# Down products as pairs of column blocks, seven products in the first chunk of each, and one hand-made order for the FFN layer of a decoder trunk

## The chip, the cores and the metric

The kernel runs on one core of a Trainium2 chip. The metric is the device time of one execution in microseconds. TensorE multiplies, VectorE and ScalarE work on tiles in SBUF and PSUM, GpSimd does a few small operations and issues the accumulating transfers, SyncE (SP) issues most loads. Each engine has its own queue of instructions and takes them in order; an instruction may first wait for counts of other engines or transfers.

## The reference

Two layers over a sequence of 256 tokens of width 2048, in float32. The first mixes with retention heads and a short convolution, the second with differential attention; each ends in a SwiGLU feed-forward layer (FFN) of hidden width 5632:

```
def swiglu(h, w_gate, w_up, w_down):
    return (jax.nn.silu(h @ w_gate) * (h @ w_up)) @ w_down
...
x = x + swiglu(rms_norm(x, norm_ffn[layer]), ffn_w_gate[layer], ffn_w_up[layer], ffn_w_down[layer])
```

## The kernel before

A float32 product is made of three float32r matmuls: each operand is split into a high part `hi` (a cast on ScalarE) and a low part `lo = src - hi` (VectorE), and hi x hi, lo x hi and hi x lo are summed in PSUM. `split_w` does it for weights, two k-tiles of 512 columns at a time (128x1024 elements), into a pool of four buffers.

The FFN runs in three parts of 4, 4 and 3 blocks of 512 hidden columns. For each part `gate_up` makes the hidden columns, then a down stage multiplies them by their rows of `w_down` and adds to `x_sb`.

`gate_up` treats gate and up weights as a 2x2 arrangement: the two token halves (a1, a2) and the two halves of a chunk of four k-tiles on one side, gate and up columns on the other. Each block of 512 columns goes through four chunks c = 0..3 of kinds 7, 8, 7, 8 (`KINDS`). In a chunk of kind 8 the four weight operands w11, w21, w12, w22 meet two activation operands each, 4 x 2 x 2 x 3 = 48 matmuls. In a chunk of kind 7 a Strassen-like scheme takes seven products (`SEVEN`), 7 x 2 x 3 = 42 matmuls, and pays with sums: of weights (t1 made by an accumulating transfer that GpSimd issues, t2, t3, t4 by VectorE, L240 to L244), of activations (s1 to s4, made once in `Stream.quad`), and of results. The results stand in PSUM tiles b1 to b7; b3 and b5 are the two banks of one tile `p35`.

Its order is written by hand (`manual_schedule`): a list of slots, one for each weight operand. In each slot the split of the operand three slots on is issued (`prepare(i + AHEAD)`), then the matmuls, then what `gather` has set for this slot: `copies`, `inner`, `gates`, `silu`, `ups` and `hidden`, which take the results to the hidden block `gs`. Eight slots after a block's last, `hidden` finishes it and appends a job; in chunk 1 of the next block the slots w21, w12 and w22 call `step()`, which moves the job on: `splits` transposes the block on TensorE and splits it from PSUM (`split4`, L361 on ScalarE, L362 on VectorE) into `hi` and `lo`, the activations of the down stage.

A down stage is four calls of `col_block`, for 512 output columns each: per k-tile, three matmuls for each token half into one of two accumulators, then `add_residual`. Nothing is summed but the accumulators. Its order, and that of all code outside `manual_schedule`, comes from a scheduler at build time. `Stream.quad` prepares a quarter of the normalized x; for the last quarter of each FFN's norm it runs as a job in chunk 1 of the first block, followed by `squares` and `scale`. Names in rows: f01 is block 1 of layer 0's FFN, 2w11 the operand w11 of its chunk 2, d00o0 column block 0 of the down stage of layer 0's part 0, n1_c3 quarter 3 of that FFN's norm.

Of the kernel before, what the change touches and what calls it, by code (L numbers as in the profile page):

```python
# [35 lines left out]
def decoder_trunk(ctx: ExitStack, tc: tile.TileContext, a: dict):  # L36
# [149 lines left out]
    def gate_up(layer, wg, wu, st, r, p0, p1, hi, lo):  # L186
# [3 lines left out]


        kinds = st.kinds
        nc_ = len(kinds)
        last7 = max(c for c, kind in enumerate(kinds) if kind == 7)
        last8 = max(c for c, kind in enumerate(kinds) if kind == 8)
        chunks = [(b, c) for b in range(p0, p1) for c in range(nc_)]
        tiles, banks, sums, begun = {}, {}, {}, set()
# [50 lines left out]
        def get_banks(b):  # L248
            nm = f"f{layer}{b}_"
            for i in (1, 2, 6, 4):  # L250
                banks[b, f"b{i}"] = acc_tile(f"{nm}p{i}")
            banks[b, "b7"] = tp_tile(nm + "p7")
            b35 = psum.tile([P, 2, NB], F32, tag="sc", name=nm + "p35")
            banks[b, "b3"], banks[b, "b5"] = b35[:, 0], b35[:, 1]
# [18 lines left out]

        later = {}

        def gather(i):


            n, b, c, operand, _ = slots[i]
            nm = f"f{layer}{b}"  # L280

            def at(k, f):
                later.setdefault(i + k, []).append(f)

            if c == last7 and operand == "t3":
                u = work.tile([P, NT, NB], F32, tag="u", name=nm + "u", bufs=1)
                g = work.tile([P, NT, NB], F32, tag="gs", name=nm + "gs", bufs=1)
                sums[b] = u, g

                def copies():  # L290
                    nc.scalar.copy(u[:, 0], banks[b, "b1"])
                    nc.scalar.copy(g[:, 0], banks[b, "b1"])

                def inner():
                    nc.vector.tensor_tensor(u[:, 0], banks[b, "b6"], u[:, 0], ALU.subtract)
                    nc.vector.tensor_tensor(u[:, 1], banks[b, "b7"], u[:, 0], ALU.add)

                at(2, copies)
                at(4, inner)
            if c == nc_ - 1 and operand == "w21":  # L300
                u, g = sums[b]

                def gates():
                    nc.vector.tensor_tensor(g[:, 0], banks[b, "b2"], g[:, 0], ALU.add)
                    nc.vector.tensor_tensor(g[:, 1], banks[b, "b4"], u[:, 1], ALU.subtract)
# [590 lines left out]
```

## Time and profile before

| what | value |
|---|---|
| median of 3 runs | 2184.47 us (2183.98 to 2184.51) |
| the profiled execution | 2184.89 us, span 2183.1 us |
| busy share of the span: PE, DVE, ACT, POOL | 99%, 75%, 53%, 8% |
| matmuls and transposes on PE | 9851 records |
| granted clock over the span | 1.00 |

PE is TensorE, DVE VectorE, ACT ScalarE, POOL GpSimd. The span runs from the first to the last instruction on the core. A busy share is an average over stages; matmuls are pipelined, so a record of 0.39 us may start 0.23 us after the one ahead of it. A bracket behind a row gives the idle time of the engine before it, and what ended it.

### The profile page before, as it was taken

How to read it: one execution, taken by the hardware profiler on the slowest of the kernel's cores; microseconds unless marked ns; L12 is line 12 of the kernel's file. 1: busy time of each engine (PE TensorE's matmuls, PEld its weight loads, DVE VectorE, ACT ScalarE, POOL GpSimd, SP SyncE). 2: the span in 40 equal slices, each digit the busy share in tenths (PEclk: the TensorE clock that was granted, in tenths of full speed). 3: DMA queues.
4: the chain of work that ended last, by engine and by line, in shares of the span. 5: the costliest groups of instructions: out<-in, count | busy, mean ns of one | idle time of the engine just before them, and what ended most of it. 6: DMA issues, size and time to landing. Idle time of an engine off the chain costs nothing.

```text
span 2183.1 us, 25895 instructions
## 1 busy us (share of the span) xinstructions
PE 2166.9 (99%) x9851; PEld 1791.9 (82%) x9851; DVE 1626.9 (75%) x1742; ACT 1153.9 (53%) x1362; POOL 170.9 (8%) x148
## 2 busy tenths in 40 slices
PE   8999999999999999999999999999999999999999
PEld 6888888788888888888888888887888888888887
DVE  5555556899669985798577787678996699857984
ACT  5444446656446653555455554466664456635552
POOL 1110000000000000000032143000000000000000
PEclk9999999999999999999999999999999999999999
DMA  8555547576566766676465555475766677666762
GB/s 292 174 170 178 193 173 250 183 246 221 198 212 205 250 215 193 216 213 223 134 197 174 175 173 174 155 247 179 250 214 209 201 214 250 206 197 212 224 214 95
DMA packets 224832, 441.99 MB, mean 202 GB/s; under 512 B 8044, under 2 KB 11588, under 8 KB 224580
## 3 DMA queue, kind: packets, MB, share of 16 engines
q1 hardware_dynamic: 209904, 414.34, 55.2%
q0 software_dynamic: 11968, 23.07, 6.8%
q10 hardware_dynamic: 2836, 2.93, 0.4%
q8 instruction: 77, 1.26, 0.2%
q14 instruction: 47, 0.39, 0.1%
HBM read 438.22 MB, written 2.10 MB: 202 GB/s over the span
## 4 chain that ended last, share of the span: by engine, by line
PE 98%; DMA 1%; DVE 1%; ACT 0%; SPq 0%; issue 0%; ACTq 0%
PE f_p L272 14%; PE f_p L270 14%; PE f_p L271 14%; PE aq_a L172 1%; PE av_a L170 1%; PE av_a L172 1%; PE ak_a L171 1%; PE av_a L171 1%; PE n3o_a L172 1%; PE ak_a L172 1%; PE n3o_a L170 1%; PE n3o_a L171 1%; PE n1o_a L172 1%; PE n1o_a L170 1%; PE ak_a L170 1%; PE d00o_a L170 1%
## 5 line engine op out<-in xcount | busy, mean ns | idle before, releaser
L270 PE MATMUL f_p<-f_1w_hi,n_hi 128*128 128x512 f32 x264 | 104.4, 395 | 0.0
L214 POOL DMA_DIRECT2D f_0y<-in_ffn_w_gate_dram x22 | 26.6, 1210 | 980.4 <-DVE n1o_lo L164 190.1
L272 PE MATMUL f_p<-f_1w_lo,n_hi 128*128 128x512 f32 x264 | 103.0, 390 | 0.0
L271 PE MATMUL f_p<-f_1w_hi,n_lo 128*128 128x512 f32 x264 | 102.8, 390 | 0.0
L270 PE MATMUL f_p<-f_3w_hi,n_hi 128*128 128x512 f32 x264 | 102.7, 389 | 0.0
L271 PE MATMUL f_p<-f_3w_hi,n_lo 128*128 128x512 f32 x264 | 102.7, 389 | 0.0
L272 PE MATMUL f_p<-f_3w_lo,n_hi 128*128 128x512 f32 x264 | 102.7, 389 | 0.0
L179 ACT CAST f_2w_hi<-f_2x 128x1024 fp32r<-128x1024 f32 x44 | 46.5, 1056 | 72.4 <-PE f_p L271 49.1
L179 ACT CAST f_0w_hi<-f_0x 128x1024 fp32r<-128x1024 f32 x44 | 46.5, 1056 | 70.9 <-PE f_p L271 50.9
L179 ACT CAST f_0t_hi<-f_0x 128x1024 fp32r<-128x1024 f32 x44 | 46.5, 1056 | 43.3 <-PE f_p L271 31.5
L164 DVE TENSOR_TENSOR d10o_lo<-d10o_raw,d10o_hi 128x1024 fp32r<-128x1024 f32 x32 | 39.2, 1225 | 37.0 <-ACT d10o_hi L162 37.0
L164 DVE TENSOR_TENSOR d00o_lo<-d00o_raw,d00o_hi 128x1024 fp32r<-128x1024 f32 x32 | 39.2, 1224 | 37.0 <-ACT d00o_hi L162 37.0
L164 DVE TENSOR_TENSOR d01o_lo<-d01o_raw,d01o_hi 128x1024 fp32r<-128x1024 f32 x32 | 39.2, 1224 | 37.0 <-ACT d01o_hi L162 37.0
L164 DVE TENSOR_TENSOR d11o_lo<-d11o_raw,d11o_hi 128x1024 fp32r<-128x1024 f32 x32 | 39.2, 1224 | 37.0 <-ACT d11o_hi L162 37.0
L181 DVE TENSOR_TENSOR f_2w_lo<-f_2x,f_2w_hi 128x1024 fp32r<-128x1024 f32 x44 | 53.8, 1223 | 14.4 <-ACT f_2w_hi L179 14.4
L181 DVE TENSOR_TENSOR f_3w_lo<-f_3y,f_3w_hi 128x1024 fp32r<-128x1024 f32 x44 | 51.9, 1221 | 13.7 <-ACT f_3w_hi L179 13.7
L181 DVE TENSOR_TENSOR f_0w_lo<-f_0x,f_0w_hi 128x1024 fp32r<-128x1024 f32 x44 | 53.6, 1218 | 11.1 <-ACT f_0w_hi L179 11.1
L162 ACT CAST d10o_hi<-d10o_raw 128x1024 fp32r<-128x1024 f32 x32 | 33.7, 1054 | 51.9 <-PE d10o_a L171 46.5
L162 ACT CAST d00o_hi<-d00o_raw 128x1024 fp32r<-128x1024 f32 x32 | 33.7, 1054 | 51.9 <-PE d00o_a L171 46.5
L162 ACT CAST d11o_hi<-d11o_raw 128x1024 fp32r<-128x1024 f32 x32 | 33.7, 1054 | 51.9 <-PE d11o_a L171 46.5
L162 ACT CAST d01o_hi<-d01o_raw 128x1024 fp32r<-128x1024 f32 x32 | 33.7, 1054 | 51.8 <-PE d01o_a L171 46.5
L164 DVE TENSOR_TENSOR n1o_lo<-n1o_raw,n1o_hi 128x1024 fp32r<-128x1024 f32 x32 | 39.1, 1223 | 29.3 <-ACT n1o_hi L162 29.3
(710 smaller groups left out, 7291.8 us busy)
## 6 DMA issues: line engine op xcount, KB each, us to landing
f_0y<-in_ffn_w_up_dram SPq DMA_DIRECT2D x22, 1024.0 KB, 6.3
f_0x<-in_ffn_w_gate_dram SPq DMA_DIRECT2D x22, 1024.0 KB, 6.6
f_1y<-in_ffn_w_up_dram SPq DMA_DIRECT2D x22, 1024.0 KB, 5.1
f_1x<-in_ffn_w_gate_dram SPq DMA_DIRECT2D x22, 1024.0 KB, 6.0
f_2y<-in_ffn_w_up_dram SPq DMA_DIRECT2D x22, 1024.0 KB, 6.1
f_2x<-in_ffn_w_gate_dram SPq DMA_DIRECT2D x22, 1024.0 KB, 5.8
f_3y<-in_ffn_w_up_dram SPq DMA_DIRECT2D x22, 1024.0 KB, 5.1
f_3x<-in_ffn_w_gate_dram SPq DMA_DIRECT2D x22, 1024.0 KB, 6.0
```

The source lines that it names most:

```text
L162: nc.scalar.copy(whi, part)
L164: nc.vector.tensor_tensor(wlo, part, whi.bitcast(F32), ALU.subtract)
L170: nc.tensor.matmul(acc[t], lhsT=hi[:, k, ts], rhs=whi[:, j], start=first, stop=False)
L171: nc.tensor.matmul(acc[t], lhsT=lo[:, k, ts], rhs=whi[:, j], start=False, stop=False)
L172: nc.tensor.matmul(acc[t], lhsT=hi[:, k, ts], rhs=wlo[:, j], start=False, stop=last)
L179: nc.scalar.copy(whi, src)
L181: nc.vector.tensor_tensor(wlo, src, whi.bitcast(F32), ALU.subtract)
L214: nc.gpsimd.dma_start(y[:, 0:KC], rows(wg, KC), accum_op=ALU.add)
L270: nc.tensor.matmul(acc, lhsT=ahi[:, j], rhs=whi[:, j], start=first, stop=False)
L271: nc.tensor.matmul(acc, lhsT=alo[:, j], rhs=whi[:, j], start=False, stop=False)
L272: nc.tensor.matmul(acc, lhsT=ahi[:, j], rhs=wlo[:, j], start=False, stop=last and j == KC - 1)
```

## The change

The down stages of parts 0 and 1 of both layers, and that of part 2 of the last layer, are no longer made by `col_block`. A down stage is now two objects `Down`, q = 0 and 1, each for two blocks of 512 output columns side by side: the left columns c0, the right ones c1. They go through the same slots as `gate_up`, now `run(pairs)` over one list of all `GateUp` and `Down` pairs of a layer, so that the order of a whole FFN layer is made by hand (part 2 of layer 0 still ends in `col_block`). Chunk 0 of a `Down` is of kind 7, the others have eight products in the form `PLAIN`: left columns into b2 and b4, right columns into b3 and b8, where b8 is the tile of b1, used anew. `first`, `inner` and `outer` take the seven products of chunk 0 to `x_sb` in the wake of that chunk, `left` and `right` the sums at the end.

Chunk 0 needs sums of activations: for the first hidden block of each paired part `splits_sums` takes the place of `splits`. It copies the transposed block to `xg`, and then `split_sums` makes three sums and, in place, s1 (a21 isn't used in a chunk of kind 7), and splits both. For it `step()` is called in two more slots, w11 and w21 of chunk 2. `Stream.quad` uses the same `split_sums`, so the sums d now come ahead of the split of x. The stores of the last part are issued by `left` and `right`, on ScalarE's queue. Buffers of the junk tile of squares go from two to one in the FFN.

```diff
+    PLAIN = (
+        ("w11", (("b2", "a11"), ("b4", "a21"))), ("w21", (("b2", "a12"), ("b4", "a22"))),
+        ("w12", (("b3", "a11"), ("b8", "a21"))), ("w22", (("b3", "a12"), ("b8", "a22"))),
+    )
...
+        def get_banks(self):
+            for i in (1, 2, 6, 4):
+                self.banks[f"b{i}"] = acc_tile(f"{self.name}p{i}")
+            self.banks["b7"] = tp_tile(self.name + "p7")
+            b35 = psum.tile([P, 2, NB], F32, tag="sc", name=self.name + "p35")
+            self.banks["b3"], self.banks["b5"] = b35[:, 0], b35[:, 1]
+            self.banks["b8"] = self.banks["b1"]
...
+    class Down(Pair):
+
...
+            c0, c1 = slice(2 * q * NB, (2 * q + 1) * NB), slice((2 * q + 1) * NB, (2 * q + 2) * NB)
+            super().__init__(f"{name}{q}_", wd[:, c0], wd[:, c1], row0, kinds, blocks)
+            self.c0, self.c1, self.done = c0, c1, done
+
+        def forms(self, c):
+            return SEVEN if self.kinds[c] == 7 else PLAIN
+
+        def gather(self, c, operand, at):
+            banks, c0, c1 = self.banks, self.c0, self.c1
+            if c == 0 and operand == "t2":
+                self.u = work.tile([P, NT, NB], F32, tag="t2", name=self.name + "u", bufs=1)
+            u = getattr(self, "u", None)
+
+            def add(t, cs, bank):
+                nc.vector.tensor_tensor(x_sb[:, t, cs], bank, x_sb[:, t, cs], ALU.add)
+
+            def first():
+                nc.scalar.copy(u[:, 0], banks["b1"])
+                add(0, c0, banks["b1"])
+
+            def inner():
+                nc.vector.tensor_tensor(u[:, 0], banks["b6"], u[:, 0], ALU.subtract)
+                nc.vector.tensor_tensor(u[:, 1], banks["b7"], u[:, 0], ALU.add)
+
+            def outer():
+                nc.vector.tensor_tensor(x_sb[:, 1, c0], x_sb[:, 1, c0], u[:, 1], ALU.subtract)
+                for t in range(NT):
+                    nc.vector.tensor_tensor(u[:, t], banks["b5"], u[:, t], ALU.add)
+                nc.vector.tensor_tensor(x_sb[:, :, c1], x_sb[:, :, c1], u, ALU.add)
+
+            def left():
+                add(0, c0, banks["b2"])
+                add(1, c0, banks["b4"])
+                if self.done:
+                    self.done(c0)
+
+            def right():
+                add(0, c1, banks["b3"])
+                add(1, c1, banks["b8"])
+                if self.done:
+                    self.done(c1)
+
...
+            if c == 0:
+                if operand == "t2":
+                    at(2, first)
+                elif operand == "t3":
+                    at(3, inner)
+                elif operand == "t1":
+                    at(3, outer)
+            elif c == len(self.kinds) - 1:
+                if operand == "w21":
+                    at(1, left)
+                elif operand == "w22":
+                    at(1, right)
+
...
+    def run(pairs):
+
+
+        chunks = [(p, c) for p in pairs for c in range(len(p.kinds))]
+        tiles, ready, later, slots = {}, {}, {}, []
+        for n, (p, c) in enumerate(chunks):
...
                     prepare(i + AHEAD)
                 multiply(i)
-                gather(i)
+                p.gather(c, operand, lambda k, f, i=i: later.setdefault(i + k, []).append(f))
                 for f in later.pop(i, ()):
                     f()
-                if kinds[c] == 8 and n % nc_ == 1 and operand != "w11":
+                if (c == 1 and operand != "w11") or (c == 2 and operand in ("w11", "w21")):
                     step()
...
+    def split_sums(xg, hi, lo, k0, kind, nm, htag, ltag, stage):
+
+
+        n = 3 if kind == 7 else 2
+        d = work.tile([P, n, KC, P], F32, tag=stage, name=nm + "sum", bufs=1)
+        if kind == 7:
+            nc.vector.tensor_tensor(d[:, 1], xg[:, K1, T1], xg[:, K1, T0], ALU.subtract)
+            nc.vector.tensor_tensor(d[:, 0], xg[:, K2, T1], d[:, 1], ALU.subtract)
+            nc.vector.tensor_tensor(d[:, 2], xg[:, K2, T0], d[:, 0], ALU.subtract)
+            nc.vector.tensor_tensor(xg[:, K1, T1], xg[:, K1, T1], xg[:, K2, T1], ALU.subtract)
+        else:
+            nc.vector.tensor_tensor(
+                d.rearrange("p i k s -> p (i k) s"), xg[:, :, T0], xg[:, :, T1], ALU.subtract
+            )
+        ks = slice(k0, k0 + KD)
+        nc.scalar.copy(hi[:, ks], xg)
+        nc.vector.tensor_tensor(lo[:, ks], xg, hi.bitcast(F32)[:, ks], ALU.subtract)
+        sh = work.tile([P, n, KC, P], F32R, tag=htag, name=nm + "_sh", bufs=1)
+        sl = work.tile([P, n, KC, P], F32R, tag=ltag, name=nm + "_sl", bufs=1)
+        nc.scalar.copy(sh, d)
+        nc.vector.tensor_tensor(sl, d, sh.bitcast(F32), ALU.subtract)
+        return sh, sl
...
@@ -412,38 +526,13 @@
                     k = KD * c + 2 * q + j
                     g = gcol[:, self.g0 + k : self.g0 + k + 1]
...
+            self.sums[c] = split_sums(
+                xg, self.hi, self.lo, KD * c, self.kinds[c], nm, f"sh{c}", f"sl{c}", "gs"
+            )
...
 
+    def splits_sums(srcs, hi, lo, sums, name):
+
+        xg = None
+        for t in range(NT):
+            yield
+            if t == 0:
+                xg = work.tile([P, KD, S], F32, tag="u", name=name + "xg", bufs=1)
+            transpose4(srcs[t], xg, t, f"{name}{t}")
+        yield
+        sums.extend(split_sums(xg, hi, lo, 0, 7, name, "hs", "hl", "gs"))
...
+        pairs = []
         for part, (p0, p1) in enumerate(((0, 4), (4, 8), (8, 11))):
             hi, lo = act_pair(KT, "act", f"h{layer}{part}")
-            gate_up(layer, wg, wu, st, r, p0, p1, hi, lo)
             nk, row0 = 4 * (p1 - p0), p0 * NB
-            if part < 2:
-                out_proj(f"d{layer}{part}", wd, nk, hi, lo, 0, row0, stream=False)
-            elif after is not None:
-                res = out_proj(f"d{layer}b", wd, nk, hi, lo, after, row0)
-            else:
-                for c in range(4):
-                    acc = col_block(f"d{layer}b{c}", wd, row0, c * NB, nk, hi, lo)
-                    add_residual(acc, c)
-                    for t in range(NT):
-                        nc.scalar.dma_start(
-                            a["out"][0, t * P : (t + 1) * P, c * NB : (c + 1) * NB],
-                            x_sb[:, t, c * NB : (c + 1) * NB],
-                        )
+            paired = part < 2 or after is None
+            sums = []
+
+            def done(b, g, hi=hi, lo=lo, p0=p0, paired=paired, sums=sums):
+                g = g[:, 0], g[:, 1]
+                if paired and b == p0:
+                    return splits_sums(g, hi, lo, sums, f"h{layer}{b}")
+                return splits(g, hi, lo, 4 * (b - p0), f"h{layer}{b}")
+
+            for b in range(p0, p1):
+                pairs.append(GateUp(layer, b, wg, wu, st, r, partial(done, b)))
+            if paired:
+                kinds = (7,) + (8,) * (p1 - p0 - 1)
+
+                def blocks(c, hi=hi, lo=lo, kinds=kinds, sums=sums):
+                    return act_blocks(hi, lo, KD * c, kinds[c], sums if kinds[c] == 7 else None)
+
+                for q in range(2):
+                    pairs.append(Down(f"d{layer}{part}", q, wd, row0, kinds, blocks, None if part < 2 else store))
+        run(pairs)
+        if after is not None:
+            res = out_proj(f"d{layer}b", wd, nk, hi, lo, after, row0)
         return res
+
```

What this does to the order, at three places. Line numbers from here to the end of this section are those of the changed kernel where a row stands under "now"; d000 is the first `Down` of layer 0, part 0, and its tile p35 holds b3 and b5. A bracket names the engines whose counts an instruction waits for.

TensorE in chunk 1 of d000, slots w21 to w22 and the two behind them; L402 multiplies hi x hi, L403 lo x hi, L404 hi x lo. Now:

```order
L402 MATMUL d000_p2_4205<-d000_1w21_hi_4268,h00_hi_2827 128x512 [waits Activation_49]
...
L404 MATMUL d000_p2_4205<-d000_1w21_lo_4270,h00_hi_2827 128x512 [waits DVE_49]
...
L402 MATMUL d000_p35_4209<-d000_1w12_hi_4278,h00_hi_2827 128x512 [waits DVE_49,Activation_49]
L403 MATMUL d000_p35_4209<-d000_1w12_hi_4278,h00_lo_2828 128x512
L404 MATMUL d000_p35_4209<-d000_1w12_lo_4280,h00_hi_2827 128x512
...
L402 MATMUL d000_p35_4209<-d000_1w22_hi_4290,h00_hi_2827 128x512 [waits Activation_49]
L403 MATMUL d000_p35_4209<-d000_1w22_hi_4290,h00_lo_2828 128x512
L404 MATMUL d000_p35_4209<-d000_1w22_lo_4292,h00_hi_2827 128x512
...
L404 MATMUL d000_p2_4205<-d000_2w11_lo_4315,h00_hi_2827 128x512
...
L402 MATMUL d000_p2_4205<-d000_2w21_hi_4333,h00_hi_2827 128x512 [waits Activation_49]
...
L404 MATMUL d000_p2_4205<-d000_2w21_lo_4335,h00_hi_2827 128x512 [waits DVE_49]
```

At this place before, in the first column block of the same stage:

```order
L170 MATMUL d00o0_a0_4165<-d00o0_hi2_4185,h00_hi_2827 128x512 [waits Activation_49]
L171 MATMUL d00o0_a0_4165<-d00o0_hi2_4185,h00_lo_2828 128x512
L172 MATMUL d00o0_a0_4165<-d00o0_lo2_4187,h00_hi_2827 128x512 [waits DVE_49]
L170 MATMUL d00o0_a0_4165<-d00o0_hi2_4185,h00_hi_2827 128x512
L171 MATMUL d00o0_a0_4165<-d00o0_hi2_4185,h00_lo_2828 128x512
L172 MATMUL d00o0_a0_4165<-d00o0_lo2_4187,h00_hi_2827 128x512
```

Where each slot waited for its own cast and its own low part, the first matmul of w12 now carries the wait for VectorE, and the low parts of w12, w22 and the next w11 carry none.

VectorE at the same place, from the split of 1w21 to that of 2w21; L302 is `first`'s addition, L309 and L310 are `inner`, L268 `hidden`, L313 to L316 `outer`. Now:

```order
L302 TENSOR_TENSOR x_sb_76<-d000_p1_4204,x_sb_76 128x512 [waits Activation_49]
L182 TENSOR_TENSOR d000_1w21_lo_4270<-d000_1x_4080,d000_1w21_hi_4268 128x1024 [waits PE_49,Activation_49]
L182 TENSOR_TENSOR d000_1w12_lo_4280<-d000_1y_4081,d000_1w12_hi_4278 128x1024 [waits DMAHW4_49,PE_49,Activation_49]
L309 TENSOR_TENSOR d000_u_4239<-d000_p6_4206,d000_u_4239 128x512
L310 TENSOR_TENSOR d000_u_4239<-d000_p7_4208,d000_u_4239 128x512 [waits DVE_49]
L182 TENSOR_TENSOR d000_1w22_lo_4292<-d000_1y_4081,d000_1w22_hi_4290 128x1024 [waits PE_49,Activation_49]
...
L182 TENSOR_TENSOR d000_2w11_lo_4315<-d000_2x_4128,d000_2w11_hi_4313 128x1024 [waits DMAHW7_49,PE_49,Activation_49]
L313 TENSOR_TENSOR x_sb_76<-x_sb_76,d000_u_4239 128x512 [waits DVE_49]
L315 TENSOR_TENSOR d000_u_4239<-d000_p35_4209,d000_u_4239 128x512
L315 TENSOR_TENSOR d000_u_4239<-d000_p35_4209,d000_u_4239 128x512 [waits DVE_49]
L316 TENSOR_TENSOR x_sb_76<-x_sb_76,d000_u_4239 128x2x512 [waits DVE_49]
L182 TENSOR_TENSOR d000_2w21_lo_4335<-d000_2x_4128,d000_2w21_hi_4333 128x1024 [waits PE_49,Activation_49]
```

In the dots stand two rows of `hidden` of block f03; the second `Down` of a stage has none there. Before, VectorE had in a column block:

```order
L164 TENSOR_TENSOR d00o0_lo8_4253<-d00o0_raw8_4249,d00o0_hi8_4251 128x1024 [waits DMAHW4_49,PE_49,Activation_49]
L164 TENSOR_TENSOR d00o0_lo10_4269<-d00o0_raw8_4249,d00o0_hi10_4267 128x1024 [waits PE_49,Activation_49]
L164 TENSOR_TENSOR d00o0_lo12_4287<-d00o0_raw12_4283,d00o0_hi12_4285 128x1024 [waits DMAHW5_49,PE_49,Activation_49]
...
L164 TENSOR_TENSOR d00o0_lo14_4303<-d00o0_raw12_4283,d00o0_hi14_4301 128x1024 [waits PE_49,Activation_49]
...
L477 TENSOR_TENSOR x_sb_76<-d00o0_a0_4165,x_sb_76 128x512 [waits PE_49]
L477 TENSOR_TENSOR x_sb_76<-d00o0_a1_4166,x_sb_76 128x512 [waits PE_49]
```

The splits keep their places, and seven operations of `first`, `inner` and `outer` now stand between those of chunk 1.

VectorE in chunk 2 of block f01, at the job of block f00; L447 to L461 are `split_sums`. Now:

```order
L182 TENSOR_TENSOR f01_2t3_lo_3379<-f01_2x_3131,f01_2t3_hi_3377 128x1024 [waits PE_49,Activation_49]
L447 TENSOR_TENSOR h00sum_3387<-h00xg_3347 128x256 [waits PE_49]
L448 TENSOR_TENSOR h00sum_3387<-h00xg_3347,h00sum_3387 128x256 [waits DVE_49]
L449 TENSOR_TENSOR h00sum_3387<-h00xg_3347,h00sum_3387 128x256 [waits DVE_49]
L450 TENSOR_TENSOR h00xg_3347<-h00xg_3347 128x2x128
L457 TENSOR_TENSOR h00_lo_2828<-h00xg_3347,h00_hi_2827 128x1024 [waits Activation_49]
L461 TENSOR_TENSOR h00_sl_3395<-h00sum_3387,h00_sh_3394 128x768 [waits Activation_49]
L182 TENSOR_TENSOR f01_2t4_lo_3400<-f01_2x_3131,f01_2t4_hi_3398 128x1024 [waits PE_49,Activation_49]
```

Before:

```order
L181 TENSOR_TENSOR f01_2t2_lo_3352<-f01_2t2_3312,f01_2t2_hi_3350 128x1024 [waits Activation_49]
L244 TENSOR_TENSOR f01_2x_3127<-f01_2t2_3312,f01_2x_3127 128x1024 [waits DVE_49]
L362 TENSOR_TENSOR h00_lo_2828<-h001_tp_3367,h00_hi_2827 128x4x128 [waits Activation_49]
L181 TENSOR_TENSOR f01_2t3_lo_3376<-f01_2x_3127,f01_2t3_hi_3374 128x1024 [waits Activation_49]
L181 TENSOR_TENSOR f01_2t4_lo_3386<-f01_2x_3127,f01_2t4_hi_3384 128x1024 [waits PE_49,Activation_49]
```

Six operations now stand between the splits of t3 and t4, where none stood; the two L362 of block f00 are gone.

## Rows read from the trace of the kernel before

**Rows 1.** The page: its head, and the chain's shares by engine.
```profile
span 2183.1 us, 25895 instructions
...
PE 98%; DMA 1%; DVE 1%; ACT 0%; SPq 0%; issue 0%; ACTq 0%
```

**Rows 2.** Windows: one gate-and-up block, one down stage; busy us (instructions), granted clock, DMA.
```profile
487.60:529.30 41.70, 41.70 (x190) 34.50 (x189) 39.43 (x40) 25.74 (x28) 1.93 (x2) 1.00 0.73 225
553.25:640.20 86.95, 86.95 (x389) 72.11 (x388) 49.06 (x47) 34.71 (x34) 2.40 (x2) 1.00 0.63 199
```

**Rows 3.** Timeline of TensorE in the down stage: start, length, instruction.
```profile
553.25 0.39 PE L170 MATMUL d00o_a<-d00o_hi,h_hi 128*128 128x512 f32 x1
...
555.97 0.39 PE L170 MATMUL d00o_a<-d00o_hi,h_hi 128*128 128x512 f32 x1
```

**Rows 4.** Timeline of VectorE in block f01 and the start of f02.
```profile
451.03 2.36 DVE L181 TENSOR_TENSOR f_2t_lo<-f_2x,f_2t_hi 128x1024 fp32r<-128x1024 f32 x2 [0.23 <-ACT f_2t_hi L179]
453.31 1.22 DVE L181 TENSOR_TENSOR f_2t_lo<-f_2y,f_2t_hi 128x1024 fp32r<-128x1024 f32 x1
...
461.37 0.68 DVE L295 TENSOR_TENSOR f01u<-f_p,f01u 128x512 f32<-128x512 f32 x1
...
462.70 1.22 DVE L181 TENSOR_TENSOR f_0w_lo<-f_0x,f_0w_hi 128x1024 fp32r<-128x1024 f32 x1
...
471.96 0.68 DVE L317 TENSOR_TENSOR f01u<-f_p,f01u 128x512 f32<-128x512 f32 x1
472.57 0.68 DVE L318 TENSOR_TENSOR f01u<-f_p,f01u 128x512 f32<-128x512 f32 x1
...
483.16 1.22 DVE L181 TENSOR_TENSOR f_2w_lo<-f_2x,f_2w_hi 128x1024 fp32r<-128x1024 f32 x1
```

**Rows 5.** Timeline of VectorE at the norm's sums (four additions, then a subtraction).
```profile
367.82 0.42 DVE L423 TENSOR_TENSOR n_c2sum<-n_c2xg 128x256 f32<-128x256 f32 x1
...
369.29 1.22 DVE L417 TENSOR_TENSOR n_lo<-n_c2xg,n_hi 128x1024 fp32r<-128x1024 f32 x1
```

**Rows 6.** Timeline of TensorE: t4 of f01's chunk 2; f02's first matmul, first of w12.
```profile
454.76 0.39 PE L270 MATMUL f_p<-f_2t_hi,n_hi 128*128 128x512 f32 x1
...
469.72 0.39 PE L270 MATMUL f_p<-f_0w_hi,n_hi 128*128 128x512 f32 x1
...
484.68 0.39 PE L270 MATMUL f_p<-f_1w_hi,n_hi 128*128 128x512 f32 x1
```

**Rows 7.** Timeline of ScalarE, TensorE and VectorE: one slot of the down stage.
```profile
558.66 1.05 ACT L162 CAST d00o_hi<-d00o_raw 128x1024 fp32r<-128x1024 f32 x1 [1.62 <-PE d00o_a L171]
...
558.69 0.39 PE L170 MATMUL d00o_a<-d00o_hi,h_hi 128*128 128x512 f32 x1
...
559.75 1.23 DVE L164 TENSOR_TENSOR d00o_lo<-d00o_raw,d00o_hi 128x1024 fp32r<-128x1024 f32 x1 [0.69 <-ACT d00o_hi L162]
```

**Rows 8.** Timeline of ScalarE and its queue: a store of two issues, the next cast.
```profile
2162.68 1.06 ACTq L666 DMA_DIRECT2D out_dram<-x_sb  x2
2165.22 1.05 ACT L162 CAST d1b_hi<-d1b_raw 128x1024 fp32r<-128x1024 f32 x1 [1.71 <-PE d1b_a L171]
```

**Rows 9.** Timeline of TensorE and ScalarE at the norm's last quarter, chunk 2 of f00.
```profile
405.23 0.39 PE L270 MATMUL f_p<-f_2w_hi,n_hi 128*128 128x512 f32 x1
...
411.94 0.50 PE L272 MATMUL f_p<-f_2t_lo,n_c_sh 128*128 128x512 f32 x1 [0.86 <-DVE f_2t_lo L181]
...
406.50 0.62 ACT L432 CAST n_c_sh<-n_c3sum 128x512 fp32r<-128x512 f32 x1 [1.89 <-DVE n_c3sum L427]
```

**Rows 10.** Windows and timeline of TensorE at the end and the start of the run.
```profile
2174.00:2183.00 9.00, 4.96 (x22) 3.76 (x21) 1.38 (x2) 0.00 (x0) 0.00 (x0) 0.89 0.15 58
...
2178.57 0.39 PE L172 MATMUL d1b_a<-d1b_lo,h_hi 128*128 128x512 f32 x1
...
7.56 0.78 PE L170 MATMUL rq_a<-rq_hi,n_hi 128*128 128x512 f32 x1
...
10.22 0.40 PE L172 MATMUL rq_a<-rq_lo,n_hi 128*128 128x512 f32 x1
```

More of the change, by code (lines that the diff above doesn't have):

```diff
@@ L1 @@
 import math
+from functools import partial
 from collections import deque
@@ L184, in decoder_trunk @@
     AHEAD = 3
[L186 to L197, printed above, removed]
+    SEVEN = (
+        ("w11", (("b1", "a11"),)), ("w21", (("b2", "a12"),)), ("t2", (("b6", "s2"),)), ("t3", (("b7", "s3"),)),
+        ("t4", (("b4", "a22"),)), ("t1", (("b5", "s1"),)), ("w22", (("b3", "s4"),)),
+    )
@@ L246, in prepare @@
                 load(n + 3)
[L248 to L254, printed above, removed]
         def multiply(i):
-            n, b, c, operand, products = slots[i]
+            n, p, c, operand, products = slots[i]
             whi, wlo = ready.pop(i)
-            a = st.blocks(c)
-            if (b, "b1") not in banks:
-                get_banks(b)
+            a = p.blocks(c)
+            if not p.banks:
+                p.get_banks()
             for bank, act in products:
                 ahi, alo = a[act]
-                acc = banks[b, bank]
-                last = (last7 if bank in ("b1", "b6", "b7") else nc_ - 1) == c
-                last = last and (kinds[c] == 7 or operand in ("w21", "w22"))
+                acc = p.banks[bank]
+                last = p.last[bank] == i
                 for j in range(KC):
-                    first = (b, bank) not in begun
-                    begun.add((b, bank))
+                    first = bank not in p.begun
+                    p.begun.add(bank)
                     nc.tensor.matmul(acc, lhsT=ahi[:, j], rhs=whi[:, j], start=first, stop=False)
@@ L272, in multiply @@
                     nc.tensor.matmul(acc, lhsT=ahi[:, j], rhs=wlo[:, j], start=False, stop=last and j == KC - 1)
[L274 to L305, printed above, removed]
-                def silu():
-                    for t in range(NT):
-                        nc.scalar.activation(g[:, t], g[:, t], AF.Silu, scale=r[:, t : t + 1])
-                at(0, gates)
-                at(6, silu)
-            if c == nc_ - 1 and operand == "w22":
-                u, g = sums[b]
-                def ups():
-                    nc.vector.tensor_tensor(u[:, 1], banks[b, "b5"], u[:, 1], ALU.add)
-                    nc.vector.tensor_tensor(u[:, 0], banks[b, "b5"], u[:, 0], ALU.add)
-                    nc.vector.tensor_tensor(u[:, 0], banks[b, "b3"], u[:, 0], ALU.add)
-                def hidden():
-                    for t in range(NT):
-                        nc.vector.scalar_tensor_tensor(
-                            g[:, t], u[:, t], r[:, t : t + 1], g[:, t], op0=ALU.mult, op1=ALU.mult
-                        )
-                    jobs.append(splits((g[:, 0], g[:, 1]), hi, lo, 4 * (b - p0), f"h{layer}{b}"))
-                at(1, ups)
-                at(8, hidden)
         with tc.manual_schedule():
@@ L335, in gate_up @@
                 prepare(i)
[L336 removed]
+            for i, (n, p, c, operand, _) in enumerate(slots):
                 if i + AHEAD < len(slots):
```

159 lines of the change are left out of this document (99 added, 60 removed).

## The prediction

> **What bounds the kernel now.** I read the chain of work that ended last first: TensorE carries 98% of it [rows 1]. Then the windows: in a whole gate-and-up block and in a whole down stage TensorE is busy in every microsecond, at granted clock 1.00 (its 2.4 GHz level), and the two stages differ in VectorE: 39.43 of 41.70 us busy in the block, 49.06 of 86.95 in the down stage [rows 2]. So time is saved by fewer matmuls, and lost wherever TensorE is made to wait, which in a block costs VectorE only 2.3 us of slack. The timeline gives the price of a matmul: twelve of 128x512 in 2.72 us, 0.2267 each [rows 3]. I call six or twelve matmuls on one split weight operand a slot, and count chunks of four k-tiles from c = 0; a slot of a seven-product chunk lasts 1.36 us, one of an eight-product chunk 2.72.
>
> **Matmuls removed.** A down stage of 16 k-tiles had 16 x 2 x 3 x 4 = 384 matmuls and has 2 x (42 + 3 x 48) = 372; the last one, of 12 k-tiles, goes from 288 to 276. Five stages lose 12 each: 60 x 0.2267 = **-13.6 us**. The transposes stay as many.
>
> **Sums of the first hidden block (five times).** In chunk 2 of the next block, VectorE's queue gets four additions of 128x256, a wait for ScalarE's cast of the result, and two subtractions, all between the splits of t3 and t4 (second place in the order). From rows of the same spot in block f01: the t3 split starts at 451.03 and two splits take 2.28 [rows 4], so the additions could start at 452.17. Four such additions run in 1.47 [rows 5]; the last ends near 453.7. The 128x1024 cast takes 1.05 [rows 7], so the subtraction of `lo` starts at 454.8 and hands on 1.14 later. The 128x768 subtraction isn't in the trace: it lies between 0.68 (128x512) and 1.22 (128x1024) [rows 4, 5]; I take 0.95, 0.87 until the next starts. Then t4's split, 1.22 long, ends at 458.05; its cast, behind the two of the sums, near 456.5. TensorE starts t4 at 454.76 [rows 6] and needs that low part two matmuls later, at 455.21: it waits 2.84 in two pieces, 1.8 for the cast and 1 for the split, with the semaphore 2.9 (bounds 2.4 and 3.3). It gives **+14.5**. The two subtractions for `lo` from PSUM that the block drops here stand before the t3 split and save nothing, since that split waits for its cast.
>
> **The wait in the down pair.** b3 and b5 are the halves of one two-bank tile. Before, VectorE read them only after all products of a block. Now `outer` reads b5 in the first chunk's wake while b3 still collects products. The order shows what comes of it (first place): TensorE's first matmul of chunk 1's w12 names a VectorE wait, the low parts of w12, w22 and the next w11 name none, that of the next w21 does again. So the count that w12 waits for lies behind the split of 2w11, and the only reads of that tile there are the two L315 rows: TensorE stops until `outer` has read b5.
>
> Where VectorE then is, in the first pair of a stage: the block-to-block seam has the same queue, chunk 0's splits and the previous block's `ups` and `hidden`. There the 2w11 split starts at 483.16 [rows 4], where the block's chunk 0 began at 469.72 and w12 of its chunk 1 at 484.68 [rows 6]. The down pair puts ahead of that split `first`'s addition (0.61, the step from 471.96 to 472.57) and `inner` (1.33, from 461.37 to 462.70): 485.10. Behind it come the split (1.14), L313 and one L315 (0.61 each), and the second L315 (0.68): done at 488.14. TensorE wants w12 at 484.68 on this clock and waits 3.46. Five first pairs: **+17.3**.
>
> In the second pair nothing is left over from a block. The split of 2w11 is tied to a weight buffer that the slot before frees: in the down stage the cast starts with the slot and the split 1.09 later [rows 7]. 1.09 + 1.14 + 0.61 + 0.61 + 0.68 = 4.13, the slot lasts 2.72: 1.4 us, four times: **+5.6**.
>
> In the last pair of layer 1 ScalarE also stores the columns of the pair before, two issues behind `left` and two behind `right`; two issues take 1.06 [rows 8], and the casts of t2 to t4 queue behind them, which in turn wait for VectorE's additions. Before, such a pair fell into a stretch in which ScalarE waited for TensorE anyway. From t3's split: 1.14 + 0.61 + 0.68, issues 1.06, cast 1.05, split 1.22 is 5.8 us between the starts of t3's split and the end of t4's, where TensorE allows about 1.4 + 1.2 and a lead of some 1.6. I take 2.4 for t4 and, VectorE being late behind it, 2.6 for the w12 wait: **+5.0** (bounds 3 and 7).
>
> **The sums of the norm's last quarter (twice).** Before, the low part of x stands ahead of the difference d, so ScalarE's cast of d waits 1.89 for it, and the cast of t2's weights behind it is late: the low part of t3 starts at 411.94, 20 matmuls after 405.23, where 409.76 was due, 2.18 lost [rows 9]. Now d comes first. I take back 1.7 of the 2.18 (bounds 0 and 2.2), since the squares still stand in ScalarE's queue there: **-3.4**.
>
> **Transfers.** Each down pair adds a 0.5 MB accumulating transfer on GpSimd's queue, issued two chunks (over 20 us) before the sum that reads it, as in a block; SP's loads come as far ahead. I cost them at nothing; if that cover went, t2's sum would be late next.
>
> **The clock.** The trace shows what a long pause does: the last matmul starts at 2178.57, and in the 9 us window to 2183 the granted clock averages 0.89 [rows 10]. At the two levels that is 2 us at 1.2 GHz, so the clock fell some 2 us after the last matmul ended. The 3.4 us waits are longer than that. At the start, with matmuls twice as far apart, six steps take 2.66 us instead of 1.36 [rows 10]; so I charge 1.3 for each fall. A pause of 0.86 us inside the run is followed by no fall [rows 9]. Five falls: **+6.5** (bounds 0 and 15.6, a fall at each of twelve pauses). The Trainium skill (TensorE: Matmul & The Clock Gate, Part 1) states that the array drops to 1.2 GHz after an idle stretch and comes back after sustained work. The end of the run agrees. By that rule the long waits fall and the short ones don't; by the run's inner rows alone, none does and the sum is 6.5 lower.
>
> **Sum.** -13.6 + 14.5 + 17.3 + 5.6 + 5.0 - 3.4 + 6.5 = +31.9, on the profiled execution's 2184.89: 2216.8. The median of the runs lies 0.4 below that execution, so **2216.4 us**.
>
> **Rivals.** (1) The clock holds through the 3.4 us waits: +25.4, 2209.9. For it: granted clock 1.00 in every window inside the run; against: the fall at the end. (2) It also falls at the 2.9 us waits and in the last pair: 12 falls, 2225.5. Against: these pauses come in two pieces with matmuls between.
> (3) The other side: b3 doesn't wait for b5. Place: the first matmul of w12 in chunk 1 of each down pair. Without it only the sums, t4 in the last pair and the quarter remain: -13.6 + 14.5 + 2.4 - 3.4 = -0.1, 2184.4. It decides if `outer` has read b5 within 14.96 us of a pair's start; by the rows it needs 18.4. The Trainium skill (PSUM — Partial Sum Buffer, Terms) speaks for it: an engine collides with another only in the same bank and quadrant, and b3 and b5 are two banks; hardware alone would ask no wait. But the instruction carries one, and no run here shows TensorE passing a named wait.
> (4) VectorE isn't late anywhere: only matmuls and the quarter count, -17.0, 2167.5. Against: 2.3 us of slack in a block [rows 2]. (5) Accumulating transfers land late in ten more chunks: 2230 or more; against: their lead.
>
> **Chances.** My forecast 0.45, rival 1 0.30, rival 2 0.14, rival 3 0.06, rival 4 0.03, rival 5 0.02. The range 2206 to 2228 holds the first three with the bounds of their terms; the forecast's own is 2211 to 2221. A measurement tells 0.2% (4.4 us) from no change: faster 0.03, same 0.06, slower 0.91.
>
> **What would show it.** Right: TensorE idle 3 to 4 us before chunk 1's w12 in each first down pair, released by the second L315, about 1.4 in second pairs; idle in two pieces of 1.8 and 1 us at t4 of chunk 2 in f01, f05, f11, f15 and f19; n_c3's idle cut to about half a microsecond; matmuls 0.45 apart behind the long waits. Wrong: no TensorE idle at w12, or a release by a transfer, or matmuls 0.227 apart straight after each wait.

## The result, and the profile of the changed kernel

The changed kernel takes 2233.17 us (median of 4 runs, 2232.47 to 2235.28) against 2184.47 before: ratio 1.0225, 95% interval 1.0213 to 1.0237. The forecast was slower, 2216.4, with a range to 2228: the sign was right, the time 5 us past the range. The profiled execution took 2232.47, 47.6 more than that of before, where the sum had 31.9.

The page, its head and the chain's shares by engine:

```profile
span 2230.6 us, 26124 instructions
...
PE 2177.1 (98%) x9791; PEld 1792.4 (80%) x9791; DVE 1745.8 (78%) x1892; ACT 1194.8 (54%) x1412; POOL 182.8 (8%) x158
...
PE 91%; DVE 6%; ACT 1%; issue 1%; DMA 1%; SPq 0%; ACTq 0%; DVEq 0%
```

VectorE now holds 6% of the chain, where TensorE had all but 2% of it [rows 1]; so TensorE waits for it. TensorE's waits (total us, times, longest):

```profile
PE d_p L402 <- DVE d_u L315: 24.8, 10, 3.4
PE f_p L402 <- ACT f_2t_hi L180: 9.0, 5, 1.8
PE f_p L404 <- DVE f_2t_lo L182: 4.8, 7, 0.9
...
PE d_p L402 <- ACT d_0t_hi L180: 1.4, 1, 1.4
...
PE d_p L404 <- DVE d_0t_lo L182: 0.5, 1, 0.5
```

The ten w12 waits, the five t4 waits in two pieces and the last pair are all there, released as forecast (two of the seven L404 waits are the norm's quarter). Their idle time is near 40 us, and the forecast had 42.4 for them. What is behind them shows in the timeline of TensorE at t4 of f01, then at w12 of d000 (a first pair) and of d001 (a second pair):

```profile
452.02 0.39 PE L404 MATMUL f_p<-f_2t_lo,n_c_sh 128*128 128x512 f32 x1
454.22 0.50 PE L402 MATMUL f_p<-f_2t_hi,n_hi 128*128 128x512 f32 x1 [1.81 <-ACT f_2t_hi L180]
454.55 0.40 PE L403 MATMUL f_p<-f_2t_hi,n_lo 128*128 128x512 f32 x1
455.81 0.50 PE L404 MATMUL f_p<-f_2t_lo,n_hi 128*128 128x512 f32 x1 [0.86 <-DVE f_2t_lo L182]
...
456.61 0.51 PE L404 MATMUL f_p<-f_2t_lo,n_hi 128*128 128x512 f32 x1
456.91 0.63 PE L402 MATMUL f_p<-f_2t_hi,n_hi 128*128 128x512 f32 x1
457.34 0.63 PE L403 MATMUL f_p<-f_2t_hi,n_lo 128*128 128x512 f32 x1
...
460.25 0.39 PE L404 MATMUL f_p<-f_2w_lo,n_c_sh 128*128 128x512 f32 x1
...
570.31 0.39 PE L404 MATMUL d_p<-d_1w_lo,h_hi 128*128 128x512 f32 x1
574.11 0.77 PE L402 MATMUL d_p<-d_1w_hi,h_hi 128*128 128x512 f32 x1 [3.41 <-DVE d_u L315]
574.67 0.63 PE L403 MATMUL d_p<-d_1w_hi,h_lo 128*128 128x512 f32 x1
575.10 0.63 PE L404 MATMUL d_p<-d_1w_lo,h_hi 128*128 128x512 f32 x1
...
621.64 0.47 PE L402 MATMUL d_p<-d_1w_hi,h_hi 128*128 128x512 f32 x1 [1.61 <-DVE d_u L315]
```

I call lost what the steps from one start to the next take beyond 0.2267 each. From 452.02 to 456.61 TensorE takes six steps in 4.59 us; six of 0.2267 are 1.36, so the two waits cost 3.23, not the 2.67 printed as idle: the time between starts also holds the ends that overlap (0.39 long, 0.2267 apart) and a slow step after each wait. Then the steps are 0.43 long up to 460.25. All 15 steps take 8.23 and should take 3.40: 4.83 lost, 1.6 of it behind the waits. In windows of 12 us around t4 of f01, and w12 of d000, d001 and d120 (the first pair of the last stage), the column after POOL is the granted clock:

```profile
452.00:464.00 12.00, 9.33 (x33) 6.90 (x32) 10.77 (x10) 9.16 (x12) 0.00 (x0) 0.86 0.60 214
570.00:582.00 12.00, 8.59 (x30) 6.54 (x29) 7.32 (x10) 2.58 (x3) 1.20 (x1) 0.72 0.88 240
617.00:629.00 12.00, 10.39 (x46) 8.30 (x45) 8.82 (x10) 4.21 (x4) 1.20 (x1) 1.00 0.84 242
2168.00:2180.00 12.00, 8.59 (x42) 6.67 (x41) 8.64 (x11) 4.09 (x5) 0.00 (x0) 1.00 0.81 244
```

0.86 and 0.72 are stretches at the 1.2 GHz level inside the window. Of the 16 places, ten have a clock below 1.00: all five t4, four of the five first w12 waits (not d120), and t4 of the last pair; none of the four second pairs. Adding up the starts in the same way at each place (where the clock fell behind a w12 wait, the wait is taken as 3.66, what the same wait cost at d120 without a fall; at t4 as the 3.23 of f01):

| place | lost, us | of it wait | of it low clock | forecast: wait, clock |
|---|---|---|---|---|
| t4, five blocks | 24.6 (4.5 to 6.0 each) | 5 x 3.23 = 16.2 | 8.4 | 14.5, 0 |
| w12, five first pairs | 26.8 (3.66 at d120, 5.2 to 6.4) | 5 x 3.66 = 18.3 | 8.5 | 17.3, 6.5 |
| w12, four second pairs | 4 x 1.85 = 7.4 | 7.4 | 0 | 5.6, 0 |
| last pair | 4.1 at t4, 1.6 at w12 | 4.1 | 1.6 | 5.0, 0 |
| norm's quarter, two | -3.5 | -3.5 | 0 | -3.4, 0 |
| 60 matmuls | -13.6 | | | -13.6 |

That is +47.4, and the spans differ by 47.5. The sum had 31.9: of the 15.5 more, 12.0 are low clock (18.5 for 6.5) and 3.6 are waits (46.0 for 42.4). So theory A: most of the time beyond the forecast is TensorE's low clock, 18.5 us in all. The rival, B: it is elsewhere (late transfers, slower stages), and a wait costs its idle time alone.

### The profile page after: what moved, and what is told of

Read it like the earlier page. It is cut to its first block, busy times and chain, and to the rows that moved or that the text cites. A ratio compares the mean times of both kernels' runs of the same rounds, so it can differ in the third digit from the quotient of the medians.

```text
span 2230.6 us, 26124 instructions
## 1 busy us (share of the span) xinstructions
PE 2177.1 (98%) x9791; PEld 1792.4 (80%) x9791; DVE 1745.8 (78%) x1892; ACT 1194.8 (54%) x1412; POOL 182.8 (8%) x158
## 4 chain that ended last, share of the span: by engine, by line
PE 91%; DVE 6%; ACT 1%; issue 1%; DMA 1%; SPq 0%; ACTq 0%; DVEq 0%
PE f_p L404 13%; PE f_p L402 13%; PE f_p L403 13%; PE d_p L402 5%; PE d_p L404 5%; PE d_p L403 5%; PE aq_a L173 1%; PE av_a L171 1%; PE av_a L173 1%; PE ak_a L173 1%; PE n3o_a L173 1%; PE ak_a L172 1%; PE n3o_a L172 1%; PE n1o_a L173 1%; PE n3o_a L171 1%; PE av_a L172 1%
## 5 line engine op out<-in xcount | busy, mean ns | idle before, releaser
L402 PE MATMUL f_p<-f_1w_hi,n_hi 128*128 128x512 f32 x264 | 104.4, 395 | 0.0
L404 PE MATMUL f_p<-f_1w_lo,n_hi 128*128 128x512 f32 x264 | 103.0, 390 | 0.0
L403 PE MATMUL f_p<-f_1w_hi,n_lo 128*128 128x512 f32 x264 | 102.8, 390 | 0.0
L402 PE MATMUL f_p<-f_3w_hi,n_hi 128*128 128x512 f32 x264 | 102.7, 389 | 0.0
L403 PE MATMUL f_p<-f_3w_hi,n_lo 128*128 128x512 f32 x264 | 102.7, 389 | 0.0
L404 PE MATMUL f_p<-f_3w_lo,n_hi 128*128 128x512 f32 x264 | 102.7, 389 | 0.0
L402 PE MATMUL d_p<-d_1w_hi,h_hi 128*128 128x512 f32 x160 | 66.9, 418 | 24.8 <-DVE d_u L315 24.8
L180 ACT CAST f_2w_hi<-f_2x 128x1024 fp32r<-128x1024 f32 x44 | 46.5, 1056 | 72.4 <-PE f_p L403 47.5
L180 ACT CAST f_0t_hi<-f_0x 128x1024 fp32r<-128x1024 f32 x44 | 46.5, 1056 | 44.0 <-PE f_p L403 31.5
L436 ACT CAST h_hi<-h_tp 128x512 fp32r<-128x512 f32 x34 | 19.8, 587 | 90.9 <-PE h_tp L433 90.9
L403 PE MATMUL d_p<-d_1w_hi,h_lo 128*128 128x512 f32 x160 | 65.6, 410 | 0.0
L404 PE MATMUL d_p<-d_1w_lo,h_hi 128*128 128x512 f32 x160 | 65.5, 410 | 0.0
L182 DVE TENSOR_TENSOR f_2w_lo<-f_2x,f_2w_hi 128x1024 fp32r<-128x1024 f32 x44 | 53.8, 1223 | 14.5 <-ACT f_2w_hi L180 14.5
L402 PE MATMUL d_p<-d_2w_hi,h_hi 128*128 128x512 f32 x160 | 62.8, 392 | 0.0
L403 PE MATMUL d_p<-d_2w_hi,h_lo 128*128 128x512 f32 x160 | 62.3, 390 | 0.0
L404 PE MATMUL d_p<-d_2w_lo,h_hi 128*128 128x512 f32 x160 | 62.3, 389 | 0.0
L369 POOL DMA_DIRECT2D f_2y<-in_ffn_w_gate_dram x22 | 26.5, 1204 | 416.1 <-DVE f_0t L381 103.0
```

The source lines that it names most:

```text
L180: nc.scalar.copy(whi, src)
L182: nc.vector.tensor_tensor(wlo, src, whi.bitcast(F32), ALU.subtract)
L369: nc.gpsimd.dma_start(y[:, 0:KC], rows(p.left, KC), accum_op=ALU.add)
L402: nc.tensor.matmul(acc, lhsT=ahi[:, j], rhs=whi[:, j], start=first, stop=False)
L403: nc.tensor.matmul(acc, lhsT=alo[:, j], rhs=whi[:, j], start=False, stop=False)
L404: nc.tensor.matmul(acc, lhsT=ahi[:, j], rhs=wlo[:, j], start=False, stop=last and j == KC - 1)
```

## The experiments

**TensorE kept at work in the waits** (`e4_fill`). Every wait stays, but the engine has matmuls by zero to do in it:

```diff
+        def fill(p, c, operand):
+            if operand == "w12" and c == 1 and p.name[0] == "d":
+                return (12, 0) if p.name == "d121_" else (28, 0) if p.name[3] == "0" else (14, 0)
...
+                nc.tensor.matmul(p.banks["b2"][:, 0:240], lhsT=zero[:, 0:P], rhs=zero, start=False, stop=False)
```

> The changed kernel with all its waits, and TensorE given matmuls with a zero operand of 240 columns right before each of them (28 before w12 in first pairs, 14 in second pairs, 16 and 6 at t4 of the blocks with sums, 12, 4 and 12 in the last pair), sized to fit into the wait; they add zero to b2. Theory A: VectorE and ScalarE are as late as before, but TensorE works on and its clock holds; the 18.5 us of low clock go, and nothing else: 2215. Rival B (the extra time isn't the clock): 2233, as without the fill, or more by what the fill overruns.

Measured 2215.03 (2213.89 to 2215.41), 18.1 less than the changed kernel. TensorE's timeline and a window at d000:

```profile
568.34 0.39 PE L421 MATMUL d_p<-d_1w_lo,h_hi 128*128 128x512 f32 x1
568.56 3.30 PE L400 MATMUL d_p<-zero 128*128 128x240 f32 x28
572.14 0.47 PE L417 MATMUL d_p<-d_1w_hi,h_hi 128*128 128x512 f32 x1 [0.28 <-DVE d_u L315]
...
567.00:579.00 12.00, 11.72 (x70) 10.12 (x69) 9.27 (x11) 2.76 (x4) 1.20 (x1) 1.00 0.94 280
```

From the last useful matmul to w12's first is 3.80 us, as without the fill (570.31 to 574.11): the wait is the same to the hundredth. Only the clock differs, 1.00 against 0.72. Over the whole run the span is 18.5 shorter than the changed kernel's, what the starts gave to the low clock. B falls.

**The waits taken away one by one.** `e1_bank` gives b3 a tile of its own, `e2_sums` spreads the sums:

```diff
+        def get_banks(self):
+            for i in (1, 2, 4, 3):
+                self.banks[f"b{i}"] = acc_tile(f"{self.name}p{i}")
+            self.banks["b6"] = tp_tile(self.name + "p6")
+            b75 = psum.tile([P, 2, NB], F32, tag="sc", name=self.name + "p75")
+            self.banks["b7"], self.banks["b5"] = b75[:, 0], b75[:, 1]
```

> Only the tiles of the down pair change: b3 gets a tile of its own, b5 shares one with b7, so TensorE's w12 in chunk 1 no longer waits for the reads of b5; the sums of the first hidden block stay where they are. Theory A (the time beyond the forecast is TensorE at its low clock behind the waits): the ten w12 places go with all that follows them, by the spacing of the matmuls in the changed kernel 26.8 us at first pairs, 7.4 at second pairs, 1.6 in the last pair, and a wait of some 0.5 us for the sums of the pair before may come at four or five seams: 2199, with no fall of the clock in a down stage. Rival B (the extra time is elsewhere, in late transfers or slower stages, and the waits cost only their idle time): 24.8 us of idle time go, 2209.

Measured 2201.68 (2196.40 to 2205.52), ratio 1.0079 (1.0063 to 1.0095). No wait at w12 is left; a window at the same place of d000:

```profile
570.00:582.00 12.00, 12.00 (x58) 9.93 (x57) 11.54 (x14) 5.33 (x7) 1.20 (x1) 1.00 1.01 285
```

31.5 us gained, more than all the idle time there (24.8), although waits at the seams between pairs came at nine places, about twice as many as expected, and take 4.8 back by the starts: A. In the profiled run, the slowest of the four, the gain is 26.9, since its clock stays low for longer at t4 of f01 and falls at one more place (last section).

```diff
-                if (c == 1 and operand != "w11") or (c == 2 and operand in ("w11", "w21")):
+                if c == 1 or (c == 2 and operand in ("w11", "w21")):
...
-        sums.extend(split_sums(xg, hi, lo, 0, 7, name, "hs", "hl", "gs"))
...
+        sub = nc.gpsimd.tensor_tensor
...
+        yield
...
+        nc.vector.tensor_tensor(lo[:, ks], xg, hi.bitcast(F32)[:, ks], ALU.subtract)
...
+        yield
+        nc.vector.tensor_tensor(sl, d, sh.bitcast(F32), ALU.subtract)
```

> Only the sums of the first hidden block change: its four subtractions of 128x256 go to GpSimd, one slot earlier, and the two subtractions for the low parts stand in two slots instead of one; the down pairs stay. Theory A: the t4 waits in f01, f05, f11, f15 and f19 go with the low clock behind them, 24.6 us by the spacing of the matmuls there: 2209, and the granted clock is 1.00 around each t4. Rival B: only 13.3 us of idle time go, 2220. If GpSimd's subtractions were too slow, t4 would still wait and the gain would be smaller than either says.

Measured 2217.39 (2215.88 to 2217.75): 15.8 gained, where A said 24.6 and B 13.3. The t4 waits shrank to three short pieces (1.92 to 1.99 lost at each place) and didn't go, so the time by itself doesn't tell them apart. The clock does: it is 1.00 around all five t4, as A said, and of the 14.7 less that the starts lose there 8.4 were low clock. A window at f01, and one at d120, which comes up in the last section:

```profile
452.00:464.00 12.00, 10.87 (x46) 8.03 (x45) 11.51 (x12) 8.67 (x11) 0.00 (x0) 1.00 0.74 251
2151.00:2163.00 12.00, 9.03 (x37) 7.14 (x36) 8.89 (x11) 3.30 (x5) 0.00 (x0) 0.86 0.84 250
```

**Both** (`e3_both`, the last pair's stores on `nc.sync`, `at(0, right)`).

> The edits of the two runs before together, with the stores of the last pair on SyncE's queue instead of ScalarE's and the last additions of a pair one slot earlier. Theory A: no pause of a microsecond is left in the FFN layers, the clock stays at 1.00, and what is left of the change is 60 matmuls fewer (-13.6) and the norm's quarter (-3.4), with 2 us of small waits: 2169, 0.7% faster than the kernel before. Rival B: the changed kernel's 40.1 us of idle time go and the rest stays: 2193, slower than the kernel before.

Measured 2180.66 (2179.57 to 2181.58), ratio 0.9983 (0.9974 to 0.9992). The clock holds, and B's 2193 is excluded, but A's 2169 is missed by almost 12. VectorE and GpSimd in block f01 say why:

```profile
446.39 1.75 DVE L182 TENSOR_TENSOR f_2t_lo<-f_2t,f_2t_hi 128x1024 fp32r<-128x1024 f32 x1 [0.84 <-ACT f_2t_hi L180]
448.06 1.76 DVE L393 TENSOR_TENSOR f_2x<-f_2t,f_2x 128x1024 f32<-128x1024 f32 x1
449.75 1.76 DVE L182 TENSOR_TENSOR f_2t_lo<-f_2x,f_2t_hi 128x1024 fp32r<-128x1024 f32 x1
451.54 1.23 DVE L630 TENSOR_TENSOR h_lo<-h00xg,h_hi 128x1024 fp32r<-128x1024 f32 x1
...
445.51 0.73 POOL L623 TENSOR_TENSOR h00sum<-h00xg 128x256 f32<-128x256 f32 x1 [0.55 <-ACT h00xg L598]
...
448.71 1.71 POOL L626 TENSOR_TENSOR h00xg<-h00xg 128x256 f32<-128x256 f32 x1
```

Beside GpSimd's subtractions VectorE's operations on 128x1024 take 1.75 instead of 1.22, three times, so the work moved off VectorE cost it 1.6 us, more than the four subtractions took there (1.47, [rows 5]). The Trainium skill (SBUF — State Buffer, SBUF: two separate sides) states that the two share one port pair, and that an operation of VectorE with two SBUF inputs locks it against one of GpSimd that reads SBUF. The trace agrees that they slow each other; GpSimd's spans are rough, so it doesn't tell whether one stops wholly.

**The sums back on VectorE** (`e5_spread`), in the 0.84 us for which it waited there:

```diff
-        yield
         d = work.tile([P, 3, KC, P], F32, tag="gs", name=name + "sum", bufs=1)
-        sub = nc.gpsimd.tensor_tensor
+        sub = nc.vector.tensor_tensor
...
         nc.scalar.copy(sh, d)
         yield
+        yield
```

> The kernel with both edits, but the four subtractions of the sums are back on VectorE, right behind the second transposed copy, where VectorE waited for ScalarE in that kernel, and the last subtraction stands two slots later. Theory A (what is left at t4 comes of GpSimd and VectorE slowing each other: a subtraction of 128x1024 took 1.75 us instead of 1.22 beside GpSimd's, and GpSimd's grew from 0.73 to 1.6): the t4 waits shrink to a few tenths and the 9.9 us lost at the five places to about 2: 2172. Rival B (the block's VectorE is full and the wait only moves on to t1 or the next split): 2180.

Measured 2171.59 (2170.86 to 2171.97), ratio **0.9940** (0.9928 to 0.9953): faster than both kernels. In f01 the four now stand between splits of full speed, and the block's window is whole:

```profile
444.50 0.42 DVE L622 TENSOR_TENSOR h00sum<-h00xg 128x256 f32<-128x256 f32 x1
...
446.09 1.22 DVE L182 TENSOR_TENSOR f_2t_lo<-f_2t,f_2t_hi 128x1024 fp32r<-128x1024 f32 x1
...
452.00:464.00 12.00, 11.92 (x53) 9.53 (x52) 11.96 (x13) 7.02 (x8) 0.00 (x0) 1.00 0.89 302
```

**Eight products instead of seven** (`e6_eight`), against `e5_spread`. `hidden` of each part's last block also comes three slots earlier; what that alone is worth wasn't tried:

```diff
-                kinds = (7,) + (8,) * (p1 - p0 - 1)
+                kinds = (8,) * (p1 - p0)
...
-                if paired and b == p0:
+                if False:
...
-                at(8, hidden)
+                at(5 if self.name in ("f03_", "f07_", "f13_", "f17_", "f110_") else 8, hidden)
```

> The same kernel, but with eight products in the first chunk of each down pair too: no sums of the first hidden block, no accumulating transfer and no combined weights in a down stage, 60 matmuls more, and the pair's first, inner and outer additions are gone. Theory A: in a kernel in which nothing waits, a product of six matmuls is worth what its matmuls take: 13.6 us longer than the kernel with seven, less the small waits that the sums still cost there (2 to 4 us): 10 to 12 us longer. Rival B (the seven-product chunk gives nothing, what it saves on TensorE is lost around it): as long as the kernel with seven.

Measured 2180.61 (2180.04 to 2183.05), ratio 0.9984 (0.9975 to 0.9993): 9.0 more than with seven, a little under what A said. The 60 matmuls should take 13.6; of the 4.6 missing, the starts in the kernel with seven show 3.7 in ten short waits at t4 and in the pairs' first chunk.

**The norm's order alone** (`e7_quarter`), in the kernel before:

```diff
-            nc.scalar.copy(self.hi[:, ks], xg)
-            nc.vector.tensor_tensor(self.lo[:, ks], xg, self.hi.bitcast(F32)[:, ks], ALU.subtract)
...
+            nc.scalar.copy(self.hi[:, ks], xg)
+            nc.vector.tensor_tensor(self.lo[:, ks], xg, self.hi.bitcast(F32)[:, ks], ALU.subtract)
             hi = work.tile([P, n, KC, P], F32R, tag=f"sh{c}", name=nm + "_sh", bufs=1)
```

> The kernel before with one thing of the change: in the sums of the norm the cast and the low part of x come behind the differences; the fourth difference stays. The forecast's term is -3.4 for both layers; by the spacing of the matmuls the changed kernel gained 1.7 at each of the two places: 2180.8. Rival: the gain comes of the dropped fourth difference and not of the order: 2183.5 or more.

Measured 2181.48 (2180.39 to 2182.99), ratio 0.9986 (0.9977 to 0.9995): -3.0. It is the order; the fourth difference stayed.

**The stores back on ScalarE's queue** (`e8_stores`: `nc.scalar.dma_start` for `nc.sync.dma_start` in `store`, against `e5_spread`).

> The kernel with VectorE's sums placed as above, but with the stores of the last pair on ScalarE's queue, as in the changed kernel. Theory A: the wait at t4 (or t3) of the last pair comes back with 2 us of idle time and, where the clock falls behind it, 1.6 more; the w12 wait doesn't, since b3 has its own tile: 2.5 to 4 us longer than with SyncE's queue. Rival B: the stores cost nothing, and the last pair waited for VectorE alone: no difference.

Measured 2175.65 (2173.96 to 2176.84), 4.1 more. Its waits:

```profile
PE d_p L410 <- ACT d_0t_hi L180: 1.6, 1, 1.6
...
PE d_p L412 <- DVE d_0t_lo L182: 0.5, 1, 0.5
```

ScalarE's casts are late behind the stores, as forecast; TensorE's starts give 2.7 at this place in the profiled run, the fastest of the five, whose clock stays at 1.00 there. Over the whole run the granted clock is 1.00 in the two fastest and 0.999 in the three slowest, so a fall behind this wait in some runs would fit; where it fell wasn't traced.

## Why the prediction was right in sign and wrong in size

- **The clock** is the step that failed: "1.3 for each fall", "Five falls: +6.5 (bounds 0 and 15.6)". It measured 18.1 with the fill and 18.5 by the starts: ten falls at some 1.8. Both factors were off. I let only the 3.4 us waits fall, because the others "come in two pieces with matmuls between"; yet at all five t4 the clock fell after two such pieces (1.81 and 0.86 of idle at f01, with two matmuls between them), and in the last pair after 1.40 and 0.52. And 1.3 was the price of six slow steps at the start of the run [rows 10]; here the slow steps run from 457 to 460 at f01, and at d000 nearly from 574 to 580. Even the upper bound, twelve falls at 1.3, was too low. Rival 2 had the mechanism and nearly the count; its 2225.5 lacked the price. The Trainium skill (TensorE: Matmul & The Clock Gate, Part 1) states that an idle stretch lowers the clock and work brings it back; the trace agrees at four of the five 3.41 us waits, and with the fill in them the clock stays at 1.00. That two short pauses do it too I had not read out of it.
- **The wait in the down pair** was right: 3.41 idle against 3.46 forecast, 1.61 against 1.4, all released by the second L315, and gone with b3's own tile. Rival 3 falls with it. By the starts the waits cost 3.66 and 1.85, so the two terms were 2.8 too small, 2.2 of it because the idle column leaves out some 0.25 per wait.
- **The sums of the first hidden block** were right in place and shape: 1.81 for the cast and 0.86 for the split (forecast 1.8 and 1); 16.2 against 14.5 for the same reason.
- **The last pair**: 4.1 of waits against 5.0, inside its bounds, with a fall that wasn't counted. Its two halves weren't as forecast: t4 cost 2.5 for 2.4, but w12 1.6 for 2.6. VectorE was not late any more at w12, it stood idle for 0.40 before the split of 2w11:

```profile
2206.66 1.23 DVE L182 TENSOR_TENSOR d_2w_lo<-d_2x,d_2w_hi 128x1024 fp32r<-128x1024 f32 x1 [0.40 <-ACT d_2w_hi L180]
```
- **The norm's quarter**: the 20 steps that lost 2.18 before [rows 9] now lose 0.44, 4.97 us for 4.53, so -3.5 at both places, against -3.4; alone it measured -3.0. TensorE in f00:

```profile
404.43 0.39 PE L402 MATMUL f_p<-f_2w_hi,n_hi 128*128 128x512 f32 x1
...
409.40 0.50 PE L404 MATMUL f_p<-f_2t_lo,n_c_sh 128*128 128x512 f32 x1 [0.28 <-DVE f_2t_lo L182]
```

- **The matmuls** went as counted: 9791 on the page, 9851 in the kernel with eight products; in the kernel whose long waits are gone, seven products in place of eight are worth 9.0 of the 13.6.
- **Transfers** cost nothing: no wait of TensorE in the FFN stages is released by one, and rival 5 falls.

## What to carry to other kernels

Cost a stall of TensorE in two parts, the starts (idle plus some 0.25 us per wait) and what the clock does behind it, and take the second from no single price: here it added two fifths to 46 us of waits. To separate the two, give the engine harmless work in the wait: if the time falls, it was the clock. Banks that are read at different times belong in different tiles, and work goes into an engine's idle gap before it goes to GpSimd.

## What was not expected of the hardware

- The same 3.41 us wait lowered the clock at four places and not at d120, where the steps behind it are 0.23 to 0.30 at clock 1.00. In `e2_sums`, where these waits are 3.0 long, it fell at all five, d120 too (0.86 in the window above). So neither the length of the pause nor the place decides it alone; what does wasn't tried.
- The four runs of `e1_bank` spread over 9.1 us, those of every other kernel over 1 to 3. Their granted clocks are 0.997, 0.995, 0.994 and 0.993 in the order of their times, from 2196.4 to 2205.5; 0.004 of the span, lost to the low clock, is 8.8 us, nearly the whole spread. So it is the falls that differ from run to run of one kernel: in the profiled run there is one even at 1097, in the stage behind layer 0's FFN (granted clock 0.86 from 1095 to 1107), where the changed kernel has 1.00. Why they differ so much in this kernel stays open.
- GpSimd's 128x256 subtraction went from 0.73 to 1.7 us beside VectorE, and VectorE's 128x1024 from 1.22 to 1.75.
